# Moving one attention tile ahead of the small tiles, and making the MLP's operand buffers slices of it

## The chip, the cores and the metric

The kernel runs on one core of one Trainium2 chip. The metric is device time in microseconds (us) of one execution. The engines are called by their names: TensorE (PE in the profile, its weight loads PEld), VectorE (DVE), ScalarE (ACT), GpSimd (POOL) and SyncE (SP, which only issues DMAs here).

## The reference

One layer of an encoder on 512 tokens of width 2048, in float32:

```
h = rms_norm(x, pre_mix_g)
a, gate, q, k, v = split(h @ w_in)                # 5 x 1024 columns
yc = silu(layer_norm(depthwise_conv31(a * sigmoid(gate)) + b_dw))
ya = neighbourhood_attention(q, k, v, rpb)        # 16 heads of 64, window 8 x 16 of an 8 x 64 grid
x = x + rms_norm(concat(yc, ya) @ w_out, post_mix_g)
h = rms_norm(x, pre_mlp_g)
x = x + rms_norm(relu(h @ w_up)**2 @ w_down, post_mlp_g)   # 8192 hidden columns
```

## The kernel before

**Number form.** Every float32 operand of a product is split in two parts of the matmul type fp32r, a high part (a rounded copy, written by ScalarE) and a low part (what is left, written by VectorE). A product is then three matmuls: high with high, high with low, low with high. A tile whose name ends in h or H is a high part, l or L a low part.

**Stages.** A list `steps` is walked in order; each step issues some twelve matmuls of 128x512 and, before and after them, whatever helper work is planned for that place. The stages are: the input projection (steps "ag", "qk" of L898 with the weights stationary and the activations `Ah`/`Al` moving, "v" of L917 to L919 the other way round); the attention, whose pieces are placed between these steps (`att_scores`, L527 and L528; the transposes, L557; `att_pv`, L571); the output projection ("out", L925 to L927, `Ah`/`Al` stationary, weights moving; at its end the sequential part "oseq", L934 to L936, whose weights all lie ready in `UH`/`UL`); a transposition into the MLP (L708) and its first step "up0" (L910 to L912); then the MLP in eight chunks of 1024 hidden columns. A chunk has 32 "up" steps (L898 again, weights stationary) and 28 "down" steps (L951 to L953: the hidden activations, in seven sums of quarters as in Strassen's scheme, are stationary as `FH`/`FL`; the weights move).

**The weight ring.** Raw weights come by DMA into four buffers `WR` (and, for down steps, four buffers `Q`). `ensure` splits them piece by piece into ring slots: `copy` writes the high part on ScalarE (L133), VectorE the low part (L212, or L215 with a gain). Up to the MLP the ring is `WH`/`WL`, 2048 columns; in the MLP it has half as much again, `WHX`/`WLX`, 1024 columns (`ring_at`). An up step takes 512 columns of the ring, a down step 1024, so in the MLP two of every six up steps, and one of every three down steps, read `WHX`/`WLX`.

**Where the tiles lie.** One pool, `sb`, holds what lives throughout, in this order: `Ah`, `Al` (32 KB per partition each), `M`, `X`, `G`, `WR`, `WH`, `WL`, then small tiles (`PRM` 304 columns, `ident` 128, `ones` 1, `rb` 512, `sm` 64). Behind it a second pool, `att`, holds `S` (14 rows of 512 columns), `KZ` (2 rows) and `U` (2560 columns). In the attention, `S` holds the queries `QS`, most of the keys (`KD`, `KL`) and the values `VC`; `KZ` holds the low parts of the keys of two heads in four; `U` holds the transposed probabilities `PTH`, `PTL`. In "oseq", `UH` is rows 0 to 7 of `S`, and `UL` is rows 8 to 11 of `S` and four rows of `U`. At the entry into the MLP `to_mlp` releases `att`, and a third pool, `mlp`, takes its place: `Q`, `FH` (2 buffers), `FL` (2), `WHX`, `WLX`. The tile framework orders accesses to what was released and to what overlaps.

**Queues.** The order on each engine is that of the program (the schedule is written out by hand). `WR` loads are issued by SyncE; the loads that add to a quarter already in `Q` or `WR` by GpSimd (L176).

Of the kernel before, what the change touches and what calls it, by code (L numbers as in the profile page):

```python
# [11 lines left out]
F32R = mybir.dt.float32r  # L12
# [4 lines left out]
P = 128  # L17
T = 512
# [47 lines left out]
def encoder_layer(ctx, tc, xT, xp, wst, pk, gmix, gmlp, rawb, maskc, out):  # L66
    nc = tc.nc
    sb = ctx.enter_context(tc.tile_pool(name="sb", bufs=1))
# [3 lines left out]

    Ah = sb.tile([P, KT, T], F32R, name="Ah")
    Al = sb.tile([P, KT, T], F32R, name="Al")
    M = sb.tile([P, 16, T], F32, name="M")
    X = [sb.tile([P, D], F32, name=f"X{j}") for j in range(4)]
    G = sb.tile([P, D], F32, name="G")
    WR = [sb.tile([P, 1024], F32, name=f"WR{i}") for i in range(NWR)]
    WH = sb.tile([P, 2048], F32R, name="WH")
    WL = sb.tile([P, 2048], F32R, name="WL")  # L80
    PRM = sb.tile([P, PK], F32, name="PRM")
    ident = sb.tile([P, P], F32, name="ident")
    ones = sb.tile([P, 1], F32, name="ones")
# [3 lines left out]
    B = [PS[:, i, :] for i in range(8)]  # L87
    x1d = drp.tile([T, D], F32, name="x1d")
    att = tc.tile_pool(name="att", bufs=1).__enter__()
    S = att.tile([P, 14, T], F32R, name="S")  # L90
    KZ = att.tile([P, 2, T], F32R, name="KZ")
    U = att.tile([P, 2560], F32R, name="U")
    junk = S[:, 12, :]

# [15 lines left out]

    UH = [S[:, i, :] for i in range(8)]
    UL = [S[:, 8 + i, :] for i in range(4)] + [U[:, 512 * i:512 * i + 512] for i in range(4)]
    QS = [S[:, i, :] for i in range(4)]
    KD = [S[:, i, :] for i in (6, 7, 12, 13)]
    KL = [S[:, 4, :], S[:, 5, :], KZ[:, 0, :], KZ[:, 1, :]]
    VC = [S[:, 8 + j, :] for j in range(4)]
    vhl = [t.rearrange("p (h w d) -> p h w d", h=4, w=2) for t in VC]
# [5 lines left out]
    f = lambda ap: ap.bitcast(F32)  # L123
# [5 lines left out]
    def dv(c):  # L129
        clk["dve"] += c  # L130

    def copy(o, i, scale=1.0):
        act(o, i, AF.Copy, scale=scale)  # L133
# [6 lines left out]
    mlp = {}  # L140

    def add_block(slot, loads):
        blocks.append(dict(slot=slot, loads=loads, sent=False))
        return len(blocks) - 1
# [50 lines left out]
    def ring_at(q):  # L195
        o, w = q["a"] % q["mod"] * 256, q["w"]
        if o < 2048:
            return WH[:, o:o + w], WL[:, o:o + w]
        o -= 2048
# [34 lines left out]
    for c in range(NCH):  # L234
# [11 lines left out]
        for i, (buf, quarters, form, signs) in enumerate(PROD):  # L246
            last = c == NCH - 1 and i == NP - 1
            fp = len(pieces)
            for nb in range(2):
                for h in range(2):  # L250
                    if buf == "q":
                        b = add_block(("q", nb, h), [(quarter(*quarters, nb, h), i > 0)])
                    else:
                        b = add_block(None, [(quarter(*x, nb, h), n_ > 0) for n_, x in enumerate(quarters)])
# [74 lines left out]
    def load_xT(b):  # L329
        if b:  # L330
            nc.scalar.dma_start(M[:, 2 * b:2 * b + 2, :], xT[b].rearrange("p (k t) -> p k t", k=2))

    a_done = [0]

    def a_prep(k):
        while a_done[0] <= min(k, KT - 1):
            i = a_done[0]
            copy(Ah[:, i, :], M[:, i, :], g1c[:, i:i + 1])
            V.scalar_tensor_tensor(Al[:, i, :], M[:, i, :], g1c[:, i:i + 1], f(Ah[:, i, :]), ALU.mult, ALU.subtract)
            dv(0.66)  # L340
            a_done[0] += 1

    nc.vector.memset(ones, 1.0)
    nc.vector.memset(f(WH[:, 1536:2048]), 0.0)
    nc.gpsimd.dma_start(PRM[:, 0:32], pk[:, 0:32])
    nc.sync.dma_start(M[:, 0, :], xT[0][:, 0:512])
    nc.scalar.dma_start(WR[0][:, 0:512], wst[0][:, 0:512])
    nc.sync.dma_start(M[:, 1, :], xT[0][:, 512:1024])
    nc.sync.dma_start(WR[0][:, 512:1024], wst[0][:, 512:1024])
    copy(sm[:, 63:64], ones)  # L350
    for i in range(7):
        mm(B[7], WH[:, 1536:1536 + P], WH[:, 1536:2048], start=True, stop=True)
    load_xT(1)
# [7 lines left out]
    def x_stat(k):  # L361
        a = tl[3]
        if k == 0:
            act(a, M[:, 0, :], AF.Square)
        else:
# [109 lines left out]
    def split_qk():  # L475
        for pr in range(2):
            q, k = tl[pr], tl[2 + pr]
            for e in range(2):
                o, x = slice(64 * e, 64 * e + 64), slice(64 - 64 * e, 128 - 64 * e)
                qs, kd = QS[2 * pr + e], KD[2 * pr + e]  # L480
                copy(qs[o], q[o])
# [37 lines left out]
    def att_scores(h):  # L519
        hl = h % 4  # L520
        for half in range(2):
            bank = B[4 + half]
            for sl, b in enumerate(((1, 0), (3, 2))[half]):
                dst = bank[:, 256 * sl:256 * sl + 256]
                tq = slice(P * b, P * b + P)
                ks = slice(64 * START[b], 64 * START[b] + 256)
                mm(dst, QS[hl][:, tq], KD[hl][:, ks], start=True, stop=False, skip_group_check=True)  # L527
                mm(dst, QS[hl][:, tq], KL[hl][:, ks], start=False, stop=True, skip_group_check=True)  # L528
# [207 lines left out]
    def to_mlp():  # L736
        att.release()
        mp = ctx.enter_context(tc.tile_pool(name="mlp", bufs=1))
        mlp["Q"] = [[mp.tile([P, 1024], F32, name=f"Q{nb}{h}") for h in range(2)] for nb in range(2)]
        mlp["FH"] = [mp.tile([P, 4, 256], F32R, name=f"FH{i}") for i in range(2)]  # L740
        mlp["FL"] = [mp.tile([P, 4, 256], F32R, name=f"FL{i}") for i in range(2)]
        mlp["WHX"] = mp.tile([P, 1024], F32R, name="WHX")
        mlp["WLX"] = mp.tile([P, 1024], F32R, name="WLX")
        cap[0] = 12

    def split_form(i):
# [20 lines left out]
    def down_pair(c, i, nb):  # L767
        return 2 * ((2 * (c % 2) + 2 * i + nb) % 4)
# [7 lines left out]
    def cunit(j, cb):  # L776
        a = CA[j // 2, cb // 2]
        o = 1024 * (cb % 2) + 512 * (j % 2)
        return a[:, o:o + 512]
# [81 lines left out]
    for si, s in enumerate(steps):  # L861
        kind, p, k = s["kind"], s["p"], s["k"]
# [7 lines left out]
        if kind == "oseq":  # L870
            ensure(p + 7 + s["j"] + 1)
        elif kind == "fin":
            ensure(p + 3)
        elif kind == "up0":
            to_mlp()
            ensure(p + 3)
        else:
            ensure(ahead(p))
            if kind == "out" and s["mode"] == "open":
                ensure(p + 3 + max(0, k - 4) * 2)  # L880
            if kind == "down" and s["c"] == NCH - 1 and s["i"] == NP - 2 and k:
                ensure(p + 3)
# [57 lines left out]
        elif kind in ("down", "fin"):  # L940
# [3 lines left out]
            for kk in range(2):  # L944
                for h, qq, tb in todo:
                    a = 2 * h + kk
# [40 lines left out]
        elif kind == "fin":  # L987
            j = s["tb"]
            m, b = cunit(j, s["nb"]), B[down_pair(s["c"], s["i"], s["nb"]) + j]
# [85 lines left out]
```

## Time and profile before

| what | value |
|---|---|
| median of 3 runs | 2090.79 us (2087.34 to 2091.76) |
| profiled execution, its own time | 2092.75 us |
| its span, first to last instruction | 2091.0 us |
| mean granted TensorE clock | 0.989 |
| TensorE busy | 2034.6 us, 97% of the span |
| VectorE busy | 1324.9 us, 63% |
| ScalarE busy | 892.7 us, 43% |
| GpSimd busy | 281.4 us, 13% |
| read from HBM | 278.42 MB, 137 GB/s over the span with what is written |

The busy time of TensorE is that in which at least one matmul is under way. Matmuls are pipelined: a record of one 128x512 matmul is some 0.39 us long, while the next starts 0.23 us after it. So the rate of a stretch is read from the starts of its first and last matmul and their number, not from the length of one.

### The profile page before, as it was taken

The page shows a single profiled execution, that of the slowest core. Times are in us where ns is not written, and L with a number is a line of the kernel's source. Part 1 is how long each engine was busy: PE and PEld are TensorE (multiplying, and loading weights), DVE is VectorE, ACT ScalarE, POOL GpSimd, SP SyncE. Part 2 cuts the span into 40 slices and gives each one's busy share as a digit, 9 for nine tenths or more (in the row PEclk, how much of TensorE's full clock was granted, in tenths as well). Part 3 has the DMA queues.
Part 4 walks back from the last instruction along what each step waited for, and adds up shares of the span by engine and source line. Part 5 has one row for each costly group of instructions (what it writes and reads, how often), then busy time and mean ns, then how long its engine had stood idle before and what let it go on. Part 6 is the DMA issues. An engine that isn't in the chain of part 4 may idle for free.

```text
span 2091.0 us, 24692 instructions
## 1 busy us (share of the span) xinstructions
PE 2034.6 (97%) x9423; PEld 1684.8 (81%) x9423; DVE 1324.9 (63%) x1656; ACT 892.7 (43%) x1387; POOL 281.4 (13%) x275
## 2 busy tenths in 40 slices
PE   9999999997999999999999999999999999999994
PEld 7888887887788888888888888888888888888873
DVE  6899896976644644534843853763673573476498
ACT  6334444435653554633433433443343343343353
POOL 5110111112101301101101100100100110110124
PEclk9999999998999999999999999999999999999997
DMA  5223232222324256735844854763763773673592
GB/s 208 97 94 107 78 97 80 94 75 69 102 85 171 91 215 157 191 122 128 197 138 123 184 161 122 175 171 102 170 191 101 158 195 111 151 190 124 136 276 81
DMA packets 78584, 288.43 MB, mean 138 GB/s; under 512 B 8880, under 2 KB 9024, under 8 KB 76672
## 3 DMA queue, kind: packets, MB, share of 16 engines
q1 hardware_dynamic: 55440, 197.16, 27.9%
q0 software_dynamic: 21008, 81.16, 20.1%
q10 hardware_dynamic: 2016, 8.53, 1.1%
q8 instruction: 74, 1.21, 0.2%
q14 instruction: 46, 0.38, 0.1%
HBM read 278.42 MB, written 8.39 MB: 137 GB/s over the span
## 4 chain that ended last, share of the span: by engine, by line
PE 68%; DVE 3%; issue 2%; ACT 1%; POOL 0%; DVEq 0%; ACTq 0%; POOLq 0%
PE PS L898 33%; PE PS L951 9%; PE PS L953 9%; PE PS L952 9%; PE PS L927 2%; PE PS L926 2%; PE PS L925 2%; DVE WL L212 1%; DVE M L822 1%; DVE M L794 0%; PE PS L708 0%; PE PS L571 0%; DVE Al L212 0%; POOL M L679 0%; PE PS L557 0%
## 5 line engine op out<-in xcount | busy, mean ns | idle before, releaser
L898 PE MATMUL PS<-Ah,WH 128*128 128x512 f32 x1176 | 462.1, 393 | 3.7 <-ACT WH L133 3.7
L898 PE MATMUL PS<-Ah,WL 128*128 128x512 f32 x1176 | 459.8, 391 | 0.0
L898 PE MATMUL PS<-Al,WH 128*128 128x512 f32 x1176 | 459.6, 391 | 0.0
L133 ACT ACTIVATE WH<-WR 128x512 fp32r<-128x512 f32 (+2 forms) x312 | 207.4, 673 | 361.3 <-PE PS L898 155.3
L212 DVE TENSOR_TENSOR WL<-WR,WH 128x512 fp32r<-128x512 f32 (+2 forms) x312 | 255.4, 828 | 166.4 <-ACT WH L133 164.2
L215 DVE SCALAR_TENSOR_TENSOR WL<-WR,PRM,WH 128x512 fp32r<-128x512 f32 x170 | 128.2, 760 | 226.2 <-ACT WH L133 226.1
L898 PEld LDWEIGHTS PS<-Ah,WH 128*128 128x128 f32 x1176 | 222.5, 189 | 50.4 <-ACT WH L133 4.4
L898 PEld LDWEIGHTS PS<-Ah,WL 128*128 128x128 f32 x1176 | 222.3, 189 | 46.8
L898 PEld LDWEIGHTS PS<-Al,WH 128*128 128x128 f32 x1176 | 222.7, 189 | 45.4
L951 PE MATMUL PS<-WH,FH 128*128 128x512 f32 x588 | 232.7, 396 | 0.0
L953 PE MATMUL PS<-WH,FL 128*128 128x512 f32 x588 | 232.5, 395 | 0.0
L952 PE MATMUL PS<-WL,FH 128*128 128x512 f32 x588 | 232.1, 395 | 0.0
L133 ACT ACTIVATE WH<-WR,PRM 128x512 fp32r<-128x512 f32 x170 | 122.9, 724 | 246.7 <-PE PS L898 227.0
L212 DVE TENSOR_TENSOR WL<-Q,WH 128x1024 fp32r<-128x1024 f32 x83 | 101.3, 1222 | 97.2 <-ACT WH L133 97.2
L133 ACT ACTIVATE WH<-Q 128x1024 fp32r<-128x1024 f32 x83 | 88.2, 1063 | 136.1 <-PE PS L953 82.0
L215 DVE SCALAR_TENSOR_TENSOR WLX<-WR,PRM,WHX 128x512 fp32r<-128x512 f32 x86 | 64.1, 751 | 121.1 <-ACT WHX L133 121.1
L176 POOL DMA_DIRECT2D Q<-in_wst_dram x96 | 86.5, 901 | 376.0 <-DVE WL L212 238.9
L176 POOL DMA_DIRECT2D WR<-in_wst_dram x32 | 28.0, 875 | 808.5 <-DMA WR<-in_wst_dram 776.4
L898 PE MATMUL PS<-Al,WHX 128*128 128x512 f32 x344 | 135.9, 395 | 0.0
L898 PE MATMUL PS<-Ah,WHX 128*128 128x512 f32 x344 | 135.9, 395 | 0.0
L898 PE MATMUL PS<-Ah,WLX 128*128 128x512 f32 x344 | 135.6, 394 | 0.0
L953 PEld LDWEIGHTS PS<-WH,FL 128*128 128x128 f32 x588 | 110.2, 187 | 27.2
(200 smaller groups left out, 3506.7 us busy)
## 6 DMA issues: line engine op xcount, KB each, us to landing
WR<-in_wst_dram SPq DMA_DIRECT2D x335, 512.0 KB, 3.5
Q<-in_wst_dram POOLq DMA_DIRECT2D x96, 512.0 KB, 5.9
Q<-in_wst_dram SPq DMA_DIRECT2D x32, 512.0 KB, 3.6
WR<-in_wst_dram POOLq DMA_DIRECT2D x32, 512.0 KB, 5.7
X<-in_xp_dram POOLq DMA_DIRECT2D x4, 1024.0 KB, 8.9
x1d<-X POOLq DMA_DIRECT2D x4, 1024.0 KB, 9.3
out_dram<-M SPq DMA_DIRECT2D x15, 256.0 KB, 2.4
M<-in_xT_dram ACTq DMA_DIRECT2D x7, 512.0 KB, 4.7
```

The source lines that it names most:

```text
L133: act(o, i, AF.Copy, scale=scale)
L176: nc.gpsimd.dma_start(t, wst[i], accum_op=ALU.add)
L212: V.tensor_tensor(l, raw, f(h), ALU.subtract)
L215: V.scalar_tensor_tensor(l, raw, q["g"], f(h), ALU.mult, ALU.subtract)
L822: V.scalar_tensor_tensor(m, m, r, x1r[j][:, cb, :], ALU.mult, ALU.add)
L898: mm(acc[n], w, (Al if t == 1 else Ah)[:, k, :], start=(k == 0 and t == 0), stop=(lastk and t == 2), skip_group_check=True)
L925: mm(acc[j], ah[:, tk], q["h"], start=st, stop=False, skip_group_check=True)
L926: mm(acc[j], ah[:, tk], q["l"], start=False, stop=False, skip_group_check=True)
L927: mm(acc[j], al[:, tk], q["h"], start=False, stop=en, skip_group_check=True)
L951: mm(B[pr + tb], fh[:, a, fs], wh, start=st, stop=False, skip_group_check=True)
L952: mm(B[pr + tb], fh[:, a, fs], wl, start=False, stop=False, skip_group_check=True)
L953: mm(B[pr + tb], fl[:, a, fs], wh, start=False, stop=en, skip_group_check=True)
```

## The change

`WH`, `WL` and `S` are allocated right behind `Ah` and `Al`, before all other tiles. `S` loses its last row (13 instead of 14), which held the high key parts of one head in four; they go to a third row of `KZ`. `KZ` and `U` stay in the pool `att`. In the MLP `FH`, `FL`, `WHX` and `WLX` are no tiles of their own any more but rows 0 to 3, 4 to 7, 8 to 9 and 10 to 11 of `S`; the pool `mlp` holds `Q` alone, on the place of `KZ` and `U`. No instruction is added, removed or moved in the program.

```diff
     Ah = sb.tile([P, KT, T], F32R, name="Ah")
     Al = sb.tile([P, KT, T], F32R, name="Al")
+    WH = sb.tile([P, 2048], F32R, name="WH")
+    WL = sb.tile([P, 2048], F32R, name="WL")
+    S = sb.tile([P, 13, T], F32R, name="S")
     M = sb.tile([P, 16, T], F32, name="M")
     X = [sb.tile([P, D], F32, name=f"X{j}") for j in range(4)]
     G = sb.tile([P, D], F32, name="G")
     WR = [sb.tile([P, 1024], F32, name=f"WR{i}") for i in range(NWR)]
-    WH = sb.tile([P, 2048], F32R, name="WH")
-    WL = sb.tile([P, 2048], F32R, name="WL")
     PRM = sb.tile([P, PK], F32, name="PRM")
...
     att = tc.tile_pool(name="att", bufs=1).__enter__()
-    S = att.tile([P, 14, T], F32R, name="S")
-    KZ = att.tile([P, 2, T], F32R, name="KZ")
+    KZ = att.tile([P, 3, T], F32R, name="KZ")
     U = att.tile([P, 2560], F32R, name="U")
...
-    KD = [S[:, i, :] for i in (6, 7, 12, 13)]
+    KD = [S[:, 6, :], S[:, 7, :], S[:, 12, :], KZ[:, 2, :]]
...
         mlp["Q"] = [[mp.tile([P, 1024], F32, name=f"Q{nb}{h}") for h in range(2)] for nb in range(2)]
-        mlp["FH"] = [mp.tile([P, 4, 256], F32R, name=f"FH{i}") for i in range(2)]
-        mlp["FL"] = [mp.tile([P, 4, 256], F32R, name=f"FL{i}") for i in range(2)]
-        mlp["WHX"] = mp.tile([P, 1024], F32R, name="WHX")
-        mlp["WLX"] = mp.tile([P, 1024], F32R, name="WLX")
+        part = lambda i, n: S[:, i:i + 2, :].rearrange("p a (b c) -> p (a b) c", c=n)
+        mlp["FH"] = [part(2 * i, 256) for i in range(2)]
+        mlp["FL"] = [part(4 + 2 * i, 256) for i in range(2)]
+        mlp["WHX"], mlp["WLX"] = [S[:, i:i + 2, :].rearrange("p a b -> p (a b)") for i in (8, 10)]
         cap[0] = 12
```

## Rows read from the trace of the kernel before

**Rows 1.** The page: span, TensorE's share, granted clock in 40 slices (tenths)

```profile
span 2091.0 us, 24692 instructions
...
PE 2034.6 (97%) x9423; PEld 1684.8 (81%) x9423; DVE 1324.9 (63%) x1656; ACT 892.7 (43%) x1387; POOL 281.4 (13%) x275
...
PEclk9999999998999999999999999999999999999997
```

**Rows 2.** Waits of TensorE: us in total, times, longest us

```profile
PE PS L952 <- DVE WLX L212: 2.0, 1, 2.0
```

**Rows 3.** Order in time, TensorE, an up stretch: start us, length us, instruction

```profile
780.77 0.39 PE L898 MATMUL PS<-Ah,WH 128*128 128x512 f32 x1
...
791.66 0.39 PE L898 MATMUL PS<-Ah,WHX 128*128 128x512 f32 x1
...
797.25 0.39 PE L898 MATMUL PS<-Ah,WH 128*128 128x512 f32 x1
```

**Rows 4.** Order in time, TensorE, the output projection

```profile
640.00 0.39 PE L925 MATMUL PS<-WH,Ah 128*128 128x512 f32 x1
...
659.27 0.39 PE L926 MATMUL PS<-WL,Ah 128*128 128x512 f32 x1
```

**Rows 5.** Order in time, TensorE, two down steps

```profile
819.18 0.39 PE L951 MATMUL PS<-WH,FH 128*128 128x512 f32 x1
...
821.98 0.39 PE L951 MATMUL PS<-WHX,FH 128*128 128x512 f32 x1
...
823.37 0.39 PE L951 MATMUL PS<-WHX,FH 128*128 128x512 f32 x1
...
824.73 0.40 PE L951 MATMUL PS<-WH,FH 128*128 128x512 f32 x1
```

**Rows 6.** Order in time, TensorE, the sequential output, first 256 tokens

```profile
699.22 0.40 PE L934 MATMUL PS<-S,Ah 128*128 128x512 f32 x1
...
710.42 1.47 PE L708 MATMUL PS<-ident,X 128*128 128x128 f32 x12
```

**Rows 7.** Order in time, TensorE, attention: P times V, and scores

```profile
194.35 1.34 PE L571 MATMUL PS<-U,S 128*128 128x256 f32 x8
195.53 0.39 PE L898 MATMUL PS<-Ah,WH 128*128 128x512 f32 x1
...
213.00 0.28 PE L527 MATMUL PS<-S 128*128 128x256 f32 x1
...
213.95 0.39 PE L898 MATMUL PS<-Ah,WH 128*128 128x512 f32 x1
```

**Rows 8.** Groups by line and shape, TensorE: count, busy us, mean ns, idle before

```profile
L898 PE MATMUL PS<-Al,WHX 128*128 128x512 f32 x344 | 135.9, 395 | 0.0
...
L951 PE MATMUL PS<-WHX,FH 128*128 128x512 f32 x292 | 115.3, 395 | 0.0
...
L557 PE MATMUL PS<-ident,X 128*128 128x128 f32 x160 | 23.2, 290 | 10.5 <-ACT X L133 10.3
...
L571 PE MATMUL PS<-U,S 128*128 128x256 f32 x64 | 10.9, 296 | 0.3 <-DVE sm L454 0.3
```

**Rows 9.** Chain that ended last, in order of time: start us, us, what

```profile
999.36 0.24 PE PS L951
...
1057.88 0.24 PE PS L951
...
2017.37 1.07 ACT WH L133
```

**Rows 10.** Busy us by stretch: PE, PEld, DVE, ACT, POOL, clock, DMA share, GB/s

```profile
985.30:1063.30 78.00, 78.00 (x338) 62.99 (x337) 60.70 (x55) 37.15 (x39) 8.74 (x10) 1.00 0.74 186
1981.10:2017.10 36.00, 36.00 (x156) 28.96 (x156) 33.80 (x31) 16.79 (x17) 5.76 (x7) 1.00 1.01 302
```

**Rows 11.** The page's groups: splitting a piece of 1,024 columns in the down steps

```profile
L212 DVE TENSOR_TENSOR WL<-Q,WH 128x1024 fp32r<-128x1024 f32 x83 | 101.3, 1222 | 97.2 <-ACT WH L133 97.2
L133 ACT ACTIVATE WH<-Q 128x1024 fp32r<-128x1024 f32 x83 | 88.2, 1063 | 136.1 <-PE PS L953 82.0
```

**Rows 12.** Order in time, ScalarE, in the up stretch of rows 3

```profile
794.43 0.72 ACT L133 ACTIVATE WHX<-WR,PRM 128x512 fp32r<-128x512 f32 x1 [2.08 <-PE PS L898]
```

## The prediction

> **What bounds the kernel now.** I read the page first: TensorE is busy for 97% of the span, and its granted clock is 0.9 or more in all slices but two [rows 1], so only the rate of the matmuls, or a hole in their stream, moves the time. The waits name no hole in the MLP worth having: the longest wait for a piece of the weight ring there is one of 2.0 us [rows 2]. So the next view is the order in time of the matmuls themselves, start against start. The stretches below lie in slices of that clock and hold no wait, and their 128x512 matmuls still come at two rates.
>
> Up step, weights from WH/WL as the stationary operand, Ah/Al moving: 48 matmuls from 780.77 to 791.66, 226.9 ns each. The next 24 are the same line with the weights in WHX/WLX: 791.66 to 797.25, 232.9 ns each [rows 3]. Output projection, stationary Ah, moving WH: 85 starts in 19.27 us, 226.7 ns each [rows 4]. Down step, stationary FH/FL, moving WH/WL: 12 in 2.80 us, 233.3 ns each. The following down step, with WHX/WLX moving, takes 2.75 us, and its last six take 1.36 us, 226.7 ns each [rows 5]. Sequential output, stationary Ah, moving S or U: 48 in 11.20 us, 233.3 ns each [rows 6].
>
> The reader is to see that no tile is slow by itself. WHX is slow with Ah and fast with FH; WH is fast with Ah and slow with FH; S and U are slow with Ah. S with U, as P times V in the attention, is fast: 8 matmuls of 2,560 columns in all take 1.18 us, and at the rate of the output projection (226.7 ns for 512 columns) they would take 1.13 us. S with KZ gives 8 matmuls of 256 columns in 0.95 us, 119 ns each [rows 7]. So a matmul has its fast rate when both operands lie in the same of two groups: {Ah, Al, WH, WL} and {S, KZ, U, FH, FL, WHX, WLX}. The groups are those of the allocation: the first stands ahead of the small tiles PRM, ident, ones, rb and sm, the second behind them. Two properties differ there: the second group lies high, and it starts behind 1216+512+4+2048+256 = 4,036 odd bytes per partition, so its offset to the first group is no multiple of a row of 512 columns (2,048 bytes). The trace holds no addresses and cannot say which of the two counts. Distance alone does not: Ah with WH has 88 KB of other tiles between Al and WH and is fast; WL and the early part of the second group are near neighbours, and that pairing is slow.
>
> **The change part by part.** S moves into the first group, ahead of the small tiles by either property. FH, FL, WHX and WLX become slices of S. KZ and U stay behind. No instruction is added or removed; the price of a mixed pair is 233.3 - 226.7 = 6.6 ns.
>
> Up steps: 3 groups of 344 matmuls have WHX or WLX as weights [rows 8]; 1,032 x 6.6 ns = 6.8 us saved. TensorE is the chain there, so all of it counts.
>
> Down steps: from 999.36 to 1057.88 lie seven times 36 matmuls, 232.2 ns each [rows 9]; three steps take 8.36 us and would take 36 x 226.7 ns = 8.16. A chunk has 28 steps, so 9.33 x 0.20 = 1.87 us; seven chunks give 13.1 us. The last chunk is set by TensorE only until 2017, where the chain passes to ScalarE and VectorE [rows 9]. Of its 36.0 us to there 2.4% or 0.85 us would go; the DMA share in it is 1.01 [rows 10], so the data may not come earlier, and I count half, 0.4 us.
>
> Down steps hold an unknown: the first six matmuls of the WHX step, a pair within one group, still take 231.7 ns [rows 5]. Either this is the crossing from mixed to pure pairs, which then vanishes, or a cost of each down step that stays: 0.03 us x 224 = 6.7 us less gain. I take the first, since the output projection has an equal step (12 matmuls, new weights each time, weights moving) and runs through at 226.7 ns [rows 4].
>
> Sequential output: 80 of its 96 matmuls move a slice of S, 80 x 6.6 ns = 0.5 us saved; the other 16 move U and stay slow. The 32 entries from a projection into an S-stationary matmul in the attention become pure as well, 0.2 us.
>
> The loss: P times V pairs stationary S with moving U, 128 matmuls (a group of 64 with 256 columns [rows 8] and one of 64 with 384); scores pair S with KZ in 48 (low key halves of two heads in four, and now the high half of one). They were pure and become mixed: 176 x 6.6 ns = 1.2 us. No row shows the price of a mixed pair at 256 or 384 columns; I bound it by nothing and by twice 6.6 ns, 0 to 2.3 us, and take 6.6 because the surcharge of a pure pair does not shrink with the columns either (the eight of 2,560 columns above lose 0.05 us against the rate of 512). The fp32 transposes pair X with ident, 224 of them (160 in the attention [rows 8] and 64 on the way into the MLP); the edit keeps X ahead of the small tiles and ident among them. I count nothing, at worst 224 x 6.6 ns = 1.5 us.
>
> Waits: Q now lies on KZ and U instead of S. Its first loads start ten steps into the up stage, and U's last reader is the sequential output that precedes it: no new wait. WHX and FH on slices of S wait for the same sequential output that their old places waited for. What could be late next is the preparation: in a down stretch VectorE is busy 60.7 of 78.0 us, ScalarE 37.2, DMA 0.74 [rows 10]; 2.4% less time leaves all of them under 0.80.
>
> Sum: 6.8 + 13.1 + 0.4 + 0.5 + 0.2 - 1.2 = 19.8 us. The profiled execution took 2092.75 us (span 2091.0), so 2073.0; the median of the runs, 2090.79, lies 1.96 lower, which gives 2071.0.
>
> A rule that speaks against this. The page "SBUF — State Buffer" of the Trainium skill, section "Who interferes with whom", says that TensorE never waits on anyone for its SBUF ports; the page "TensorE: Matmul & The Clock Gate" of the Trainium skill, section "Step-by-step: what each phase is for", adds that the weight load has a read port independent of the moving operand's. By these, it would not matter where the two lie and the sum would be 0, which is the first rival below. The trace disagrees as far as rates go: 226.7 against 233 ns with the same instruction and clock.
>
> **The rivals.** *No change.* The two rates come from something that goes with the tiles but not with their place, for instance the slot in the ring or the stage; then 2092.75 in the profile, 2090.8 as median, or 1 us more by the attention's share. For it: only two ring sizes exist and WHX is always the third slot. Against it: WHX turns fast with FH [rows 5], and S and U, in no ring, follow the same split.
>
> *Half.* Only one of the two pairings is cured, because S ahead of the small tiles is still unlike Ah or unlike WH in what counts. Then only the down steps (13.5) or only the up steps (6.8) gain: 2077 to 2084.
>
> *Slower.* FH, FL, WHX and WLX are now one tile S. If the order of accesses were kept for the tile and not for the slices, each write of WHX in a down stage would wait for all reads of FH before it, and TensorE then for the write: ScalarE and VectorE take 1.06 + 1.22 us for a piece of 1,024 columns [rows 11], so some 2.3 us in each of the 73 down steps that use WHX (292 matmuls of L951, four a step [rows 8]), +168 us: 2259. It decides from the first down step on. Against it: ScalarE writes WHX at 794.43 [rows 12] in the midst of matmuls that read WHX [rows 3], so slices of one tile are ordered apart today.
>
> **How the numbers follow.** Forecast 0.85, no change 0.08, half 0.03, slower 0.04. Predicted time 2071. Low end: no loss in the attention (+1.2), the last chunk in full (+0.4), and the lowest run shown lies 3.4 under the median: 2066. High end: the step cost stays (-6.7), attention at twice the price (-1.1), transposes (-1.5), and 1 us for the highest run: 2081. The 0.15 left out are the other cases (of "half" some lies inside). A change of 0.2%, 4 us, is about what a measurement of this kernel can tell from none. Forecast and half are faster (0.88); no change is within it (0.08); slower 0.04.
>
> **What the profile would show.** Right: up steps at 226.7 ns with WHX as with WH (384 matmuls in 87.0 us), three down steps in 8.16 us, the matmuls of the sequential output that move S at 226.7 and those that move U still at 233, P times V longer than 1.18 us by 0.05. Wrong: WHX steps still at 233 ns (no change), a first half of each down step at 232 (the step cost), or waits of TensorE on WLX or FL of 1 us and more (slower). The forecast fails too if the tail after 2017 grows by what the stages ahead of it gain.

## The result, and the profile after

The changed kernel takes 2068.48 us (median of 4 runs, 2067.04 to 2069.78), the kernel before 2090.24 us (median of 4 runs on the same chip, 2087.34 to 2091.76). The ratio is 0.9898, with a 95% interval from 0.9886 to 0.9911: 21.8 us faster. The profiled execution took 2069.47 us.

The page of after, to be read against [rows 1]: span, TensorE's line, granted clock in 40 slices.

```profile
span 2067.6 us, 24691 instructions
...
PE 2011.1 (97%) x9423; PEld 1683.7 (81%) x9423; DVE 1323.7 (64%) x1656; ACT 893.4 (43%) x1387; POOL 282.4 (14%) x275
...
PEclk9999999999999999999999999999999999999997
```

The same 9423 matmuls keep TensorE busy for 23.5 us less, at the same share of the span. (The one instruction fewer is a semaphore instruction in TensorE's queue.) The other engines' busy times hardly move. So no hole was closed; the matmuls follow each other faster. Where that happens is seen by comparing start with start in the order of time.

Order in time on TensorE, after: up steps and down steps (start us, length us, instruction), against [rows 3] and [rows 5].

```profile
777.45 0.39 PE L898 MATMUL PS<-Ah,WH 128*128 128x512 f32 x1
...
788.33 0.39 PE L898 MATMUL PS<-Ah,S 128*128 128x512 f32 x1
...
793.76 0.39 PE L898 MATMUL PS<-Ah,WH 128*128 128x512 f32 x1
...
815.52 0.39 PE L951 MATMUL PS<-WH,S 128*128 128x512 f32 x1
...
818.25 0.39 PE L951 MATMUL PS<-S 128*128 128x512 f32 x1
...
820.97 0.39 PE L951 MATMUL PS<-WH,S 128*128 128x512 f32 x1
```

What was WHX is now a slice of S. Its 24 up matmuls take 5.43 us (before 5.59), 226 ns each; the 48 with WH take 10.88, 227 ns each. A down step with WH takes 2.73 us (before 2.80), one with the weights in S 2.72 (before 2.75). One column misleads here: each matmul's own length is 0.39 us at either rate, while the next one starts after 0.23. Only the starts show the rate.

The sequential output of after, against [rows 6]: matmuls that move S from 696.60, U from 699.77, S from 702.54.

```profile
696.60 0.39 PE L934 MATMUL PS<-S,Ah 128*128 128x512 f32 x1
...
699.77 0.40 PE L936 MATMUL PS<-U,Ah 128*128 128x512 f32 x1
...
702.54 0.39 PE L936 MATMUL PS<-S,Ah 128*128 128x512 f32 x1
...
707.58 1.14 PE L708 MATMUL PS<-ident,X 128*128 128x128 f32 x9
```

The whole takes 10.98 us (before 11.20). From 696.60 come 14 matmuls in 3.17 us, 226 ns each; from 699.77 twelve in 2.77 us, 231 ns each, and that stretch holds the ones that move U, which stayed behind the small tiles.

P times V of after, against [rows 7]:

```profile
194.69 1.34 PE L571 MATMUL PS<-U,S 128*128 128x256 f32 x8
195.87 0.39 PE L898 MATMUL PS<-Ah,WH 128*128 128x512 f32 x1
```

It takes 1.18 us as before, although S and U now lie in different groups. The waits of after hold one of TensorE for VectorE's writes into S (us in total, times, longest); it answers to [rows 2]:

```profile
PE PS L952 <- DVE S L212: 2.5, 1, 2.5
```

The chain of after, up steps of the second and third chunk (start us, us):

```profile
891.85 87.04 PE PS L898 x384
...
1055.05 87.04 PE PS L898 x384
```

A chunk is 163.20 us long, from 891.85 to 1055.05. Busy time by stage, first before and then after, cut at the start of the MLP and at the start of its last chunk (columns as in [rows 10]):

```profile
0.00:741.42 741.42, 714.46 (x3704) 611.96 (x3705) 554.33 (x852) 351.95 (x733) 139.87 (x127) 0.98 0.31 106
741.42:1893.05 1151.63, 1151.63 (x5002) 937.41 (x5001) 624.93 (x644) 466.67 (x545) 98.14 (x112) 1.00 0.60 156
1893.05:2091.00 197.95, 168.51 (x721) 135.44 (x719) 145.60 (x160) 74.12 (x110) 43.39 (x36) 0.94 0.54 152
```

```profile
0.00:738.57 738.57, 712.21 (x3704) 610.43 (x3705) 553.42 (x852) 351.90 (x733) 140.49 (x127) 0.99 0.30 106
738.57:1871.05 1132.48, 1132.48 (x5002) 937.85 (x5001) 624.73 (x644) 467.27 (x545) 98.11 (x112) 1.00 0.60 159
1871.05:2067.60 196.55, 166.45 (x720) 135.44 (x719) 145.51 (x160) 74.17 (x110) 43.80 (x36) 0.94 0.52 153
```

Seven chunks of the MLP give 19.15 us of the span's 23.4, with TensorE busy throughout in both. The last chunk and the end give 1.40, the stages ahead of the MLP 2.85.

### The profile page after: what moved, and what is told of

Its sections match the earlier page's. It is cut to its first block, busy times and chain, and to the rows that moved or that the text cites. A ratio compares the mean times of both kernels' runs of the same rounds, so it can differ in the third digit from the quotient of the medians.

```text
span 2067.6 us, 24691 instructions
## 1 busy us (share of the span) xinstructions
PE 2011.1 (97%) x9423; PEld 1683.7 (81%) x9423; DVE 1323.7 (64%) x1656; ACT 893.4 (43%) x1387; POOL 282.4 (14%) x275
## 4 chain that ended last, share of the span: by engine, by line
PE 68%; DVE 3%; issue 2%; ACT 1%; POOL 0%; DVEq 0%; ACTq 0%; POOLq 0%
PE PS L898 33%; PE PS L952 9%; PE PS L953 9%; PE PS L951 9%; PE PS L927 2%; PE PS L926 2%; PE PS L925 2%; DVE WL L212 1%; DVE M L822 1%; DVE M L794 0%; PE PS L708 0%; PE PS L571 0%; DVE Al L212 0%; POOL M L679 0%; PE PS L557 0%
## 5 line engine op out<-in xcount | busy, mean ns | idle before, releaser
L133 ACT ACTIVATE WH<-WR,PRM 128x512 fp32r<-128x512 f32 x170 | 122.9, 725 | 246.0 <-PE PS L898 226.7
L952 PE MATMUL PS<-WL,S 128*128 128x512 f32 x588 | 229.0, 389 | 0.0
L953 PE MATMUL PS<-WH,S 128*128 128x512 f32 x588 | 228.8, 389 | 0.0
L951 PE MATMUL PS<-WH,S 128*128 128x512 f32 x588 | 228.8, 389 | 0.0
L898 PE MATMUL PS<-Ah,S 128*128 128x512 f32 x688 | 218.8, 389 | 0.0
L898 PEld LDWEIGHTS PS<-Ah,S 128*128 128x128 f32 x688 | 129.1, 188 | 26.8
L215 DVE SCALAR_TENSOR_TENSOR S<-WR,PRM,S 128x512 fp32r<-128x512 f32 x86 | 64.1, 751 | 115.7 <-ACT S L133 115.7
L898 PE MATMUL PS<-Al,S 128*128 128x512 f32 x344 | 133.8, 389 | 0.0
L418 DVE SCALAR_TENSOR_TENSOR M<-G,PRM,M 128x512 f32<-128x512 f32 x180 | 129.7, 751 | 0.0
```

What stands on the lines that cost most here:

```text
L215: V.scalar_tensor_tensor(l, raw, q["g"], f(h), ALU.mult, ALU.subtract)
L418: queue.append((TAP, lambda j=j, src=src, d=d: V.scalar_tensor_tensor(M[:, j, :], src, wdw[:, j, d:d + 1], M[:, j, :], ALU.mult, ALU.add)))
L898: mm(acc[n], w, (Al if t == 1 else Ah)[:, k, :], start=(k == 0 and t == 0), stop=(lastk and t == 2), skip_group_check=True)
L951: mm(B[pr + tb], fh[:, a, fs], wh, start=st, stop=False, skip_group_check=True)
L952: mm(B[pr + tb], fh[:, a, fs], wl, start=False, stop=False, skip_group_check=True)
L953: mm(B[pr + tb], fl[:, a, fs], wh, start=False, stop=en, skip_group_check=True)
```

## The experiments

The prediction left open which property of the two groups counts: that one lies high behind the small tiles (SIDE), or that the small tiles shift one against the other by an odd number of bytes (OFFSET). The prediction counts 4,036 bytes of small tiles. But the allocator starts tiles at multiples of 32 bytes, so they take 4,064, which is 32 less than 4,096. (The first run below bears this out: 4,036 and 32 would not bring the tiles into step.) All tiles of operands are multiples of 2,048 bytes long, and the slices that matmuls read start at multiples of 256, those of 512 columns at multiples of 512. So a gap of 32 bytes (8 columns) makes or ends the shift between the tiles ahead of it and those behind it, and moves nothing else.

**pad_before.** The kernel before, with 32 unused bytes behind the small tiles:

```
     sm = sb.tile([P, 64], F32, name="sm")
+    gap = sb.tile([P, 8], F32, name="gap")
```

> The kernel before with one unused tile of 8 columns (32 bytes per partition) behind the small tiles, so that S, KZ, U and the MLP's tiles start 32 bytes later and the small tiles fill 4,096 bytes instead of 4,064; every tile stays high or low where it was. Theory OFFSET (a pair of operands is slow when their starts differ by an odd multiple of 32 bytes): all pairs become even, MLP steps at 226.7 ns, sequential output wholly at 226.7 ns, time 2067 to 2071 us. Rival SIDE (a pair is slow when one operand lies high and the other low in the memory): nothing changes, 233 ns in the WHX up steps and the WH down steps, 2088 to 2092 us.

Measured: 2069.78 us (median of 4 runs), the kernel before 2090.13 (7 runs), ratio 0.9897, interval 0.9880 to 0.9913. Its order in time, two up stretches and two down steps:

```profile
807.37 0.39 PE L899 MATMUL PS<-Ah,WHX 128*128 128x512 f32 x1
...
812.81 0.39 PE L899 MATMUL PS<-Ah,WH 128*128 128x512 f32 x1
...
818.25 0.39 PE L952 MATMUL PS<-WH,FH 128*128 128x512 f32 x1
...
820.97 0.39 PE L952 MATMUL PS<-WHX,FH 128*128 128x512 f32 x1
```

WHX with Ah takes 5.44 us for 24 and WH with FH 2.72 for 12, both at the fast rate, with every tile on its old side. SIDE falls. Thirty-two unused bytes do what the whole change does.

**pad_after.** The changed kernel, with 32 bytes between WL and S, so that the neighbours are out of step again:

```
     WL = sb.tile([P, 2048], F32R, name="WL")
+    gap = sb.tile([P, 8], F32, name="gap")
     S = sb.tile([P, 13, T], F32R, name="S")
```

> The changed kernel with the unused 32 bytes between WL and S, so that S stays next to WH but 32 bytes off. OFFSET: up steps on S at 233 ns, down steps with WH at 233 ns, down steps on S alone at 227 to 229 ns, sequential output slow with S and fast with U, some 20 us more than the changed kernel, 2087 to 2091 us. SIDE: as the changed kernel, 2067 to 2070 us, all at 226.7 ns.

Measured: 2092.24 us, a single run. Order in time:

```profile
810.48 0.39 PE L899 MATMUL PS<-Ah,S 128*128 128x512 f32 x1
...
816.08 0.39 PE L899 MATMUL PS<-Ah,WH 128*128 128x512 f32 x1
...
821.53 0.39 PE L952 MATMUL PS<-WH,S 128*128 128x512 f32 x1
...
824.32 0.40 PE L952 MATMUL PS<-S 128*128 128x512 f32 x1
...
827.05 0.40 PE L952 MATMUL PS<-WH,S 128*128 128x512 f32 x1
```

S with Ah takes 5.60 us for 24 and WH with S 2.79 for 12: the slow rates are back, and so is the time of before, with the operands side by side but for 32 bytes. S with S stays fast, 2.73 for 12. The matmuls of the sequential output that move U were expected fast and are not: they come every 231 ns, among the slow ones that move S. The time lies 1 us above what was expected, no more than runs of one kernel differ.

**pad_weights.** The changed kernel, with the gap between Al and WH, so that WH, WL and S agree and Ah and Al don't:

```
     Al = sb.tile([P, KT, T], F32R, name="Al")
+    gap = sb.tile([P, 8], F32, name="gap")
     WH = sb.tile([P, 2048], F32R, name="WH")
```

> The changed kernel with the unused 32 bytes between Al and WH, so that Ah and Al are 32 bytes off everything else that is multiplied with them, and WH and S are even to each other. OFFSET: all up steps, the ag and qk projections and the output projection at 233 ns, down steps at 226.7: (3072 + 1536 + 672 + 80) x 6.6 ns = 35 us more than the changed kernel, 2101 to 2107 us; the 256-column matmuls of the v projection show the price for short ones, expected none (120 ns). SIDE: as the changed kernel, 2067 to 2070 us.

Measured: 2097.56 us, a single run. Order in time, two up stretches and a down step:

```profile
816.48 0.40 PE L899 MATMUL PS<-Ah,S 128*128 128x512 f32 x1
...
822.08 0.40 PE L899 MATMUL PS<-Ah,WH 128*128 128x512 f32 x1
...
827.67 0.40 PE L952 MATMUL PS<-WH,S 128*128 128x512 f32 x1
...
830.40 0.39 PE L952 MATMUL PS<-S 128*128 128x512 f32 x1
```

Both kinds of up matmul are slow now (24 in 5.60 or 5.59 us), and the down steps fast (2.73): which pairs are slow follows the offset pair by pair. The sum is below the expected range, and one reason is in the attention's v projection, 256 columns wide. First pad_weights, then after:

```profile
277.05 0.28 PE L918 MATMUL PS<-WH,Ah 128*128 128x256 f32 x1
...
280.20 0.28 PE L918 MATMUL PS<-WH,Ah 128*128 128x256 f32 x1
```

```profile
274.06 0.28 PE L917 MATMUL PS<-WH,Ah 128*128 128x256 f32 x1
...
277.30 0.28 PE L917 MATMUL PS<-WH,Ah 128*128 128x256 f32 x1
```

27 starts in 3.15 us, 116.7 ns each, against 3.24 us, 120.0 ns: at 256 columns the shifted pair is a little faster, not slower. Over 768 such matmuls that is 2.5 us. The chain of pad_weights (start of the MLP, and of its last chunk) places the rest:

```profile
748.56 22.39 PE PS L899 x96
...
1898.72 89.60 PE PS L899 x384
```

Seven chunks take 17.7 us longer than in after, as 7 x 384 x 6.6 ns would have it. The MLP starts 10.0 us later (738.57 in after), where the sum had 15.1; with the 2.5 above, 2.6 of that stay open. The last chunk and the end grow by 0.5, where the sum had 2.5.

**pad_all.** The changed kernel, with the gap ahead of Ah, so that everything is shifted alike:

```
+    gap = sb.tile([P, 8], F32, name="gap")
     Ah = sb.tile([P, KT, T], F32R, name="Ah")
```

> The changed kernel with the unused 32 bytes ahead of Ah, so that every tile starts 32 bytes later and all distances stay. OFFSET taken as the difference of the two operands: as the changed kernel, 2066 to 2071 us. OFFSET taken as the start of each operand against a fixed grid of 64 bytes: all matmuls of 512 columns slow or otherwise changed, 2110 us and more. SIDE: as the changed kernel.

Measured: 2069.85 us, a single run. Its chain, up steps of the second and third chunk:

```profile
894.39 87.04 PE PS L899 x384
...
1057.59 87.04 PE PS L899 x384
```

A chunk takes 163.20 us, as in after. So a shift of 32 bytes that both operands share does not count, and the reading with a fixed grid of 64 falls; the difference of the two counts.

**rows_of_64.** Is the harm in 32 bytes in particular, or would differences in steps of 64 be free? The changed kernel, with gaps of 16, 16, 48 and 96 columns, so that Ah, Al, WH, WL and S start at 0, 64, 128, 320 and 192 modulo 512 bytes:

```
+    gapAl = sb.tile([P, 16], F32, name="gapAl")
     Al = sb.tile([P, KT, T], F32R, name="Al")
+    gapWH = sb.tile([P, 16], F32, name="gapWH")
     WH = sb.tile([P, 2048], F32R, name="WH")
+    gapWL = sb.tile([P, 48], F32, name="gapWL")
     WL = sb.tile([P, 2048], F32R, name="WL")
+    gapS = sb.tile([P, 96], F32, name="gapS")
     S = sb.tile([P, 13, T], F32R, name="S")
```

> The changed kernel with unused columns ahead of Al, WH, WL and S, so that the starts lie 0 (Ah), 64 (Al), 128 (WH), 320 (WL) and 192 (S) bytes past a multiple of 512; the differences between operands are 64, 128, 192, 256 and 320 bytes. Theory GRID64 (only the difference within 64 bytes counts): as the changed kernel, every MLP step at 226.7 ns, 2066 to 2071 us. Rival GRID512 (operands must agree within a larger grid, 128 to 512 bytes): pairs with an uneven difference at 233 ns, all up steps, down steps and the output projection, up to 2068.5 + 56 = 2124 us.

Measured: 2103.04 us, a single run. Order in time, an up stretch on S:

```profile
816.05 0.39 PE L902 MATMUL PS<-Ah,S 128*128 128x512 f32 x1
...
821.61 0.39 PE L902 MATMUL PS<-Ah,WH 128*128 128x512 f32 x1
```

Its 24 matmuls take 5.56 us, 231.7 ns each, with differences of 192 bytes (Ah, S) and 128 (Al, S). A grid of 64 falls. The time stays 21 us under the rival's bound: the slow stretches come at 231 to 233 ns, 4 to 6 above the fast rate and not 6.6 throughout, and S with S keeps the fast rate.

**parts_of_64.** Differences that are no multiple of 32 either. The tiles are 16 columns longer, and slices of them are used that start 16 (WH), 8 (WL) and 40 (S) bytes in:

```
+    def at_byte(n, o, name):
+        return sb.tile([P, n + 16], F32R, name=name)[:, o // 4:o // 4 + n]
+    WH, WL = at_byte(2048, 16, "WH"), at_byte(2048, 8, "WL")
+    S = at_byte(13 * T, 40, "S").rearrange("p (a b) -> p a b", b=T)
```

(Ah and Al likewise, 0 bytes in.) The edit does more than the expectation counts: each tile is 64 bytes longer, so the next ones move by 64 each. Modulo 256 the operands start at 0 (Ah), 64 (Al), 144 (WH), 200 (WL) and 40 (S).

> The changed kernel with the starts shifted inside 64 bytes: Ah and Al 0, WH 16, WL 8, S 40 bytes. Theory HALF (a pair is slow when its operands lie in different 32-byte halves of the 64): WH and WL with Ah and Al stay at 226.7 ns in the up steps and the output projection, up steps on S and down steps with WH turn slow, 2087 to 2092 us. Rival ANY (any difference within 64 bytes costs the 6.6 ns): all 512-column pairs but S with S slow, 2068.5 + 52 to 58 us, 2120 to 2127 us. Third possibility GRADED: each difference has a rate of its own, some perhaps under 226.7 ns; the trace gives one for 8, 16, 24, 32 and 40 bytes.

Measured: 2115.94 us, a single run. Order in time, an up stretch on S, then a down step with WH and one with the weights in S:

```profile
818.95 0.40 PE L901 MATMUL PS<-Ah,S 128*128 128x512 f32 x1
...
824.54 0.39 PE L901 MATMUL PS<-Ah,WH 128*128 128x512 f32 x1
...
830.15 0.39 PE L954 MATMUL PS<-WH,S 128*128 128x512 f32 x1
...
832.92 0.40 PE L954 MATMUL PS<-S 128*128 128x512 f32 x1
...
835.72 0.40 PE L954 MATMUL PS<-WH,S 128*128 128x512 f32 x1
```

Every stretch is slow: 24 up matmuls take 5.59 us on S and 5.61 on WH, and WH with S takes 2.77 for 12. What I had not expected: S with S takes 2.80 us for 12, though their difference is nothing, against 2.73 in pad_after. Their start is now 8 bytes off a multiple of 32. Why that costs was not tried further. So the run settles less than it was made for: HALF, ANY and GRADED are not told apart, since the steps of 64 that rows_of_64 found slow are in its differences too, and S's start costs by itself.

**steps_of_128.** Is 256 bytes free? The changed kernel, with a gap of 256 bytes ahead of WH and one of 128 ahead of S:

```
+    gap0 = sb.tile([P, 64], F32, name="gap0")
     WH = sb.tile([P, 2048], F32R, name="WH")
     WL = sb.tile([P, 2048], F32R, name="WL")
+    gap1 = sb.tile([P, 32], F32, name="gap1")
     S = sb.tile([P, 13, T], F32R, name="S")
```

> The changed kernel with unused columns ahead of WH (256 bytes) and ahead of S (128 more), so that Ah and Al lie 256 bytes from WH and WL, and S 128 bytes from WH and 384 from Ah, within 512. GRID128 (differences that are a multiple of 128 are free): all at 226.7 ns, 2066 to 2071 us. GRID256: the projections and the up steps on WH at 226.7 ns, the up steps on S and the down steps with WH slower by 4 to 7 ns each, 2080 to 2091 us. GRID512: all pairs but S with S slower, 2095 to 2125 us.

Measured: 2089.87 us, a single run; the kernel before took 2092.89 on that chip (median of 7). Order in time:

```profile
807.21 0.40 PE L900 MATMUL PS<-Ah,S 128*128 128x512 f32 x1
...
812.80 0.39 PE L900 MATMUL PS<-Ah,WH 128*128 128x512 f32 x1
...
818.26 0.40 PE L953 MATMUL PS<-WH,S 128*128 128x512 f32 x1
...
821.05 0.40 PE L953 MATMUL PS<-S 128*128 128x512 f32 x1
```

Ah with S, 384 bytes, takes 5.59 us for 24 and WH with S, 128 bytes, 2.79 for 12: both slow. Ah with WH, 256 bytes, takes 5.46 for the 24 behind a slow stretch: fast but for the crossing. So of the steps tried, 256 is free, and 128 is not: GRID256 holds.

**all_even.** The changed kernel, with 32 bytes behind the small tiles, so that KZ, U and Q come into step as well. Its rival says that the attention's pairs, mixed by the change, cost 1.2 us that this gives back.

```
     sm = sb.tile([P, 64], F32, name="sm")
+    gap0 = sb.tile([P, 8], F32, name="gap0")
```

> The changed kernel with the unused 32 bytes behind the small tiles, so that KZ, U and Q come even with all the rest (differences a multiple of 512 bytes). Theory: the sixteen matmuls of the sequential output that move U go from 230 to 234 to 227 ns, 0.1 us saved; P times V and the scores lose nothing or 3 ns each of 176, at most 0.5 us; the time is that of the changed kernel within its spread, 2066 to 2071 us. Rival (the changed kernel still pays 1.2 us for its mixed pairs in the attention, as the prediction counted): 1 us less than the changed kernel, 2065 to 2069 us, and P times V back at 1.18 from 1.23 us.

Measured: 2068.06 us (median of 4 runs), the kernel before 2092.89 (7 runs), ratio 0.9894, interval 0.9874 to 0.9913. P times V in its order of time:

```profile
193.77 1.33 PE L572 MATMUL PS<-U,S 128*128 128x256 f32 x8
194.94 0.39 PE L899 MATMUL PS<-Ah,WH 128*128 128x512 f32 x1
```

1.17 us, against 1.18 with mixed pairs: the attention's price falls. The time can't be told from that of the changed kernel, and by itself, with runs 5 us apart, it could not have shown 1.2 us. No version that was tried beats the changed kernel by more than runs differ.

## Why the prediction was right, step by step

The forecast was 2071.0, in a range from 2066 to 2081; 2068.48 was measured. Its mechanism, that the rate goes with the pair of operands and where the two lie, is borne out by the runs above; only S with S in parts_of_64 shows something more.

**The MLP.** By the prediction's terms, seven chunks should give 13.1 us in the down steps and seven eighths of 6.8 in the up steps, 19.05 together; the stages above show 19.15. The last chunk and the end were to give 0.4 + 0.85, and gave 1.40.

**The unknown in the down step.** The prediction took the first six slow matmuls of a WHX step for a crossing and not for a cost of each step. It was the crossing: the whole step from 818.25 runs at 227 ns. The 6.7 us kept in the high end were not needed.

**The sequential output.** Predicted 0.5 us for both halves; one half gave 0.22, the whole 0.34, and the part with U stayed slow, as it should.

**The term that was mis-sized: the attention, -1.2 us.** The prediction carried the 6.6 ns of 512 columns over to 256 and 384. P times V shows 1.18 us mixed, 1.18 before and 1.17 in all_even, and a matmul of the v projection of pad_weights is 3.3 ns faster when shifted. At 256 and 384 columns the price is about nothing; the low bound was right. (One reading is off too, without weight in the sum: of the eight scores of [rows 7], read as S with KZ, every other one is S with S.)

**The stages ahead of the MLP.** With those terms (0.5 + 0.2 - 1.2) they were to become 0.5 us longer; in the profiles they are 2.85 shorter. Most of that is not the change. pad_before has every pair in step and still starts the MLP at 741.30 (before 741.42, after 738.57), and all_even starts it at 736.43. So this start differs by 5 us between kernels whose pairs are all fast. By an estimate, two places account for most of the 2.85 us. In a stretch of ten us the granted clock is 0.83 in the profile of before, part of it at 1.2 GHz, behind a wait of TensorE for ScalarE of 2.1 us, which is 1.7 us of work lost; in after, the same stretch is at 2.4 GHz throughout. Busy time there, before and then after:

```profile
355.00:365.00 10.00, 7.56 (x31) 5.86 (x30) 8.95 (x13) 4.84 (x12) 1.46 (x1) 0.83 0.14 52
```

```profile
355.00:365.00 10.00, 7.58 (x38) 5.92 (x37) 8.95 (x14) 4.71 (x11) 1.33 (x1) 1.00 0.16 56
```

And one of two waits of 1.0 us for VectorE's WL at line 919 is gone. pad_before has the clock of 0.83 there and the second wait too, with its pairs cured. Why they come and go was not tried. The profiled span fell by 23.4 us where the sum had 19.8; of the 3.6 between, 3.35 lie in these stages. The attention's loss that did not come is 1.2 of them, and the rest is luck, as far as the runs show.

**The rivals.** No change: the WHX steps run at 227 ns. Half: both the up and the down steps are cured. Slower by an order over the whole tile S: TensorE waits for VectorE's S once, 2.5 us, where [rows 2] had one of 2.0 us, not in each of 73 steps.

**Where the reason was too wide.** The prediction named two properties and could not tell them apart, and it compared the offset with 2,048 bytes. The runs leave only the offset, and its measure is 256, as long as the starts are multiples of 32. Had the offset been seen as the cause, the edit would have been one line of 32 bytes. The page "SBUF — State Buffer" of the Trainium skill, section "Who interferes with whom", has TensorE wait on no one for its ports. Here the rate of its matmuls still depends on where their two operands lie, 226.7 against 233.3 ns, and the measurement decides; that one of its reads holds up the other would be a guess, which no run tests.

## What to carry to other kernels

In a kernel that TensorE bounds, sort the start-to-start time of equal matmuls by their pair of operands; two rates at one granted clock, with no wait, point at the layout. Give every tile that matmuls of 512 columns read the same start modulo 256 bytes, itself a multiple of 32, by a gap behind odd small tiles or by putting those last. Measure the price at each width before carrying it over: here it was up to 6.6 ns at 512 columns and none at 256.

## What the runs showed of the hardware

A 128x512 matmul with new weights each time comes every 226.7 ns when the starts of its two operands differ by a multiple of 256 bytes and are multiples of 32. It comes every 232 to 233 ns when they differ by 32 bytes (pad_after, pad_weights) or 128 (steps_of_128). In rows_of_64, whose stretches mix 64, 128 and 192 bytes, it comes every 231 to 233 ns; 64 alone was not tried. The height in memory and the distance do not count: pad_before and pad_all are as fast as after. The cost does not grow with the difference: 32 bytes cost as much as 128. Right after a slow stretch the first few matmuls of a fast pair are still slow (231.7 ns in the first six of [rows 5]). At 256 and 384 columns a shifted pair was not slower. Whether one of TensorE's reads holds up the other, and why a pair with no difference is slow at a start of 8 modulo 32 bytes, stays open.
